# Pools by lifetime, and a later place for the forget gate's products: one edit of a hybrid attention/SSM block on one core

## The chip, the cores and the metric

The kernel runs on one core of a Trainium2 chip, as one program with one launch. A core has TensorE (PE in the profile; its weight loads are listed apart as PEld), VectorE (DVE), ScalarE (ACT), GpSimd (POOL) and SyncE (SP). SP and POOL issue most of the DMAs. The metric is device time in microseconds (us), the median over several runs of the same program; lower is better. The output has to agree with an fp32 reference.

## The reference, cut to what matters

One layer of a streaming encoder on 1024 frames of 1024 features, with 16 meta tokens put in front (1040 positions):

```python
xn = rmsnorm(h, norm_mix_g)
q, k, v, f_logit, u, gates = split(xn @ w_in, ...)    # 512, 512, 512, 8, 512, 2048 columns
y_a = forgetting_attention(q, k, v, f_logit, b_forget) @ w_attn_out
        # logit[t,s] = q_t.k_s/8 + F[t] - F[s],  F = cumsum(log_sigmoid(f_logit + b_forget))
z   = gelu(s5(u, ...))             # 32 groups of 16 channels, 64 complex states each
zg  = z @ w_glu                    # 512 -> 2048
y_s = zg[:, :1024] * sigmoid(zg[:, 1024:])
g   = sigmoid(gates)
h   = h + (g[:, :1024] * y_a + g[:, 1024:] * y_s) @ w_o
h   = h + conv_ffn(rmsnorm(h, norm_ffn_g))     # 1024 -> 2 x 2816 -> 1024, causal conv of width 3
out = rmsnorm(h, norm_final_g)[16:]
```

Everything is fp32. The edit concerns the first 300 us: the projection of `u`, the gates of the SSM branch, the SSM, the forget logits, q and k of the first head pair, and the loading of `z` for the GLU product.

## The kernel before, in words

**Products.** An fp32 operand is kept as a high part in the reduced type that PE takes at full rate and a low part with the rest; a product is three matmuls (high by high, high by low, low by high; `dense_steps`, lines 159 to 161). Features are `xhi` and `xlo`, 8 blocks of 128 features by 1040 positions. The high part is a cast or scaled copy on ACT (L369 for features, L146 and L603 for weights and z), the low part a subtraction (`split_lo`, L129, or the fused form in L370), mostly on DVE. `wchunk` (L138) streams a 1024 by 128 weight block through two buffers each of `raw`, `whi`, `wlo`; with `act=True` the cast is on ACT and the low part is made by an accumulating DMA, issued by POOL (`lo_by_dma`, L133 to 136). `seven` (L202) forms a product of 2 x 2 blocks with seven block products instead of eight; its weight forms are combined on POOL (L643) and split into buffer pairs `ops`, ten of them, that lie in the `whi`/`wlo` buffers (eight) and in the GLU's pool (two).

**Stages at issue.** (1) Normalization and `u`'s projection by four blocks of positions. The features of blocks 0 and 1 are first made without the norm's factor for `u`'s product; then `factors` and `normed_features` make the normalized ones for all blocks. `us`, four tiles of 128 channels, is scaled by the factor for the first two blocks (L436, four DVE operations) and stored to `u_d` in DRAM (L440, 32 DMAs on SP and POOL). (2) The gates of the SSM branch, chunks 8 to 15 of 16 (`gate_chunk`, `stage_gates`): 8 chunks x 3 pieces of positions x 24 matmuls = 576 matmuls; each piece is evicted with a sigmoid on ACT (L484) into a `gs` tile and stored to `g_d` by POOL (L485). (3) The SSM in four quarters of 8 groups. A quarter loads its `U` back from `u_d`, makes tables on DVE (`Vm`, `Wi`, `Gm`, `Kt`, `Tm`), multiplies `Wi` by `U` on PE (L1789), runs rotations and two scans on DVE (L1512, L1810, L1811) into states `St`, multiplies these with `Gm` and `U` with `Tm` on PE (L1830, L1832), applies the gelu on ACT and stores `Y` to `y_d` (L1835). The gate products are a generator: `advance(q)` emits them up to 288, 360, 480, 540 between the steps of the quarters, and `run(gates)` the last 36 after the SSM. (4) `forget()`: 3 pieces of 16 matmuls each, ACT copies to `fx` (L532), DVE adds into `fl_` (L533), then log sigmoid, a scan and a store. (5) `load_z`: for each quarter eight loads of `zt` from `y_d` (L598; half of the last quarter's on POOL), casts (L603) and splits into `zs`, and sums and differences `zf` on DVE and POOL (L616 to 619) whose casts and splits are the blocks T1 to T4. (6) q and k of the first head pair (`project_qk`, with `act=True`), then eight GLU blocks, each a `seven` followed by `gate`.

**Memory.** Pools are opened on a left and on a right stack of on-chip memory. A tile that lies where older tiles were waits, tile by tile, for their last users (`reuse_waits="tile"`). The SSM has one pool `sp` and an `sio` (for `sy` and `U`) on the left. `usb`, the tiles of `us`, are two in a pool `up` above and two in the `pc` slots. The gates' `gs` tiles lie on the right, in part over where `usb` lies. `forget` has a pool `fwork` on the right with `fl_` and `fx`, after the gates' pool is closed. `zt`, `zf` and the GLU's outputs share a pool `gated`, and all of z (`zs`, T1 to T3) with the GLU's work tiles a pool `glu`, both over the memory of the SSM.

**Order.** The order of the instructions on each engine isn't that of the program text: a planner simulates the kernel, and on each engine takes next what is ready by its own estimates, with the earlier in the text first. `after(inst, first)` adds an edge that fixes an order without a semaphore. The position of a step in the text is thus its priority.

The code itself:

Of the kernel before, what the change touches and what calls it, by code (L numbers as in the profile page):

```python
# [46 lines left out]
TILES = [(0, META)] + [(META + P * i, P) for i in range(SEQ // P)]  # L47


@with_exitstack  # L50
def block_kernel(ctx, tc, x, meta, xbt, x0t, g1t, w_q, w_k, w_v, w_f, w_u, w_g, b_f, w_ao, lam_d, bw_d, cw_d,
# [79 lines left out]
    late = []  # L131
# [6 lines left out]
    def wchunk(src, k, eng=None, act=False, copy=False):  # L138
# [6 lines left out]
        if act:  # L145
            S.copy(hi, raw)  # L146
            lo_by_dma(lo, hi, src)
            return hi, lo
# [17 lines left out]
    def run(gen):  # L166
        for _ in gen:
            pass
# [111 lines left out]
    sp = pool(st_s, "ssm", side="left")  # L280
    sio = pool(st_s, "ssmio", side="left")
    for tag, n, cols in (("Gm", 2, 1152), ("Tm", 2, 1024), ("Wi", 2, 1024), ("pc", 2, 2080), ("tq", 3, 1152)):
        sp.tile([P, cols], F, tag=tag, name="hold", bufs=n)
# [39 lines left out]
    for i in range(5, 9):  # L323
        load_x(i)
    us2, ul2 = (sp.tile([P, 2, n, SW if n == 2 else NCH], dt, tag="pc", name=nm, bufs=2)
                for n, dt, nm in ((CH, F, "usb"), (2, R, "ul")))
# [47 lines left out]
    def normed_features(b):  # L374
# [3 lines left out]
        return [features(b, k)[1] for k in range(KD)][-1]  # L378
# [37 lines left out]
    for b in (2, 3):  # L416
        last = normed_features(b)
# [8 lines left out]
        if b == 3:  # L426
            for q in (0, 1):
                factors(q)
            for q in (0, 1):
                normed_features(q)  # L430
# [3 lines left out]
    for m in range(4):  # L434
        ub = us[m][:, :, :rs01.shape[1] // CH]
        V.tensor_tensor(ub, ub, by_chunks(rs01), ALU.mult)  # L436
# [29 lines left out]
    split_lo(GP, wf[:, :, 32:32 + H], fraw, wf[:, :, :H])  # L466
    st_g = ExitStack()
# [4 lines left out]
    def gate_chunk(i, pl, tanh):  # L472
# [3 lines left out]
        for t, n in QBLK[::-1] if i == KD else QBLK:  # L476
# [5 lines left out]
            else:  # L482
                gs = pl.tile([P, LQ // 3], F, tag="gs", name="gs", bufs=2)
# [13 lines left out]
    BEHIND = (288, 360, 480, 540)  # L497
# [7 lines left out]

    st_x = ExitStack()
    sx = pool(st_x, "ssmx", side="left")
    begin(0)
    ssm_out(0)
    begin(1)  # L510
    for q in range(4):
        next(chains[q])
        if q < 3:
            ssm_out(q + 1, sx if q == 1 else None)
        advance(q)
        run(chains[q])
        if q < 2:
            begin(q + 2)
        if q == 1:
            next(ssm_steps)  # L520
    st_x.close()
    run(gates)
    st_g.close()
    st_s.close()
# [20 lines left out]
    fw = pool(st_f, "fwork", side="right")  # L545
    fl_, fx = (fw.tile([H, L], F, name=nm) for nm in ("fl_", "fx"))
    forget()
    st_f.close()
# [29 lines left out]
    gz = pool(st_k2, "gated", side="left")  # L578
    zp = pool(st_z, "glu", side="left")
    TH = L // 2  # L580
    NC2 = NCH // 2
    T3, T2, T1 = ([zp.tile([P, 2, TH], R, name=f"z{i}{w}") for w in "hl"] for i in (3, 2, 1))
# [1317 lines left out]
```

## Time and profile before

| what | value |
|---|---|
| median of 3 runs | 1477.25 us (1477.24 to 1478.09) |
| the profiled execution | 1479.76 us, span 1478.0 us |
| mean granted TensorE clock | 0.990 |
| PE busy | 1432.5 us (97%), 9646 matmuls |
| PEld busy | 1351.2 us (91%) |
| DVE busy | 1075.8 us (73%), 2198 instructions |
| ACT busy | 724.0 us (49%), 1419 instructions |
| POOL busy | 770.1 us (52%), 888 instructions |
| DMA | 209.31 MB, mean 142 GB/s |
| instructions | 26529 |

The profile is that of one execution. "Busy" is the time in which an engine had an instruction running. A table of windows gives for each stretch of the span the busy time and number of instructions of each engine, the granted clock of TensorE (1.00 is full), the mean busy share of the 16 DMA engines and the rate. A line of waits reads: waiting engine and line, the arrow and what released it, then total time, count and mean in us. A line of the timeline reads: start, duration, engine (SPq is SP's queue of DMA issues) and line, operation, outputs and inputs with shapes, number of instructions run together, and in brackets the idle time ahead of the first with its releaser.

### The profile page before, as it was taken

The numbers are of one execution on the slowest core, as the hardware profiler recorded it, in microseconds if no ns is written. First come the engines' busy times: TensorE is split into PE (matmuls) and PEld (weight loads), VectorE is DVE, ScalarE is ACT, GpSimd is POOL, SyncE is SP. The second block draws the span as 40 slices with busy tenths as digits, with TensorE's granted clock in tenths as the row PEclk, the third lists the DMA queues.
The fourth block names the chain that finished last, engine by engine and source line by source line (L and its number), as shares of the span: only waits on it lengthen the run. The fifth ranks groups of instructions, "written<-read, shape, count | busy, mean of one in ns | idle before, by whom it ended". The sixth has DMA issues, their size and how long they took to land. (4 is left out here: it accounts for less than half of the span.)

```text
span 1478.0 us, 26529 instructions
## 1 busy us (share of the span) xinstructions
PE 1432.5 (97%) x9646; PEld 1351.2 (91%) x9646; DVE 1075.8 (73%) x2198; ACT 724.0 (49%) x1419; POOL 770.1 (52%) x888
## 2 busy tenths in 40 slices
PE   8989997999999999999999999999999999998997
PEld 8889997998899999999879999999999999776886
DVE  7888758861657676656469977788877666788685
ACT  7556566531646565542655444444444445652433
POOL 2722128760646556515861244555544327889766
PEclk9999998999999999999999999999999999999998
DMA  8746553550027432146974255667753214866413
GB/s 309 174 116 162 140 115 100 168 159 32 25 74 197 108 80 94 44 177 237 274 156 143 66 141 145 168 174 195 185 136 107 79 69 154 306 200 168 135 40 114
DMA packets 89653, 209.31 MB, mean 142 GB/s; under 512 B 14442, under 2 KB 22266, under 8 KB 89140
## 3 DMA queue, kind: packets, MB, share of 16 engines
q1 hardware_dynamic: 70068, 162.55, 33.6%
q0 software_dynamic: 17728, 41.41, 14.5%
q10 hardware_dynamic: 1728, 3.68, 0.7%
q8 instruction: 76, 1.25, 0.4%
q14 instruction: 53, 0.43, 0.1%
HBM read 168.52 MB, written 69.35 MB: 161 GB/s over the span
## 5 line engine op out<-in xcount | busy, mean ns | idle before, releaser
L159 PE MATMUL mm<-xhi,whi 128*128 128x342 f32 (+2 forms) x480 | 157.8, 329 | 5.6 <-ACT gs L484 2.9
L161 PE MATMUL mm<-xhi,wlo 128*128 128x342 f32 (+2 forms) x480 | 156.3, 326 | 0.0
L160 PE MATMUL mm<-xlo,whi 128*128 128x342 f32 (+2 forms) x480 | 155.8, 325 | 0.0
L1135 POOL TENSOR_TENSOR ov<-ov,og 128x1024 f32<-128x1024 f32 x21 | 51.1, 2434 | 121.8 <-ACT og L1134 117.9
L129 DVE TENSOR_TENSOR sw<-sf,sw 128x512 fp32r<-128x512 f32 x72 | 66.7, 927 | 50.4 <-ACT sw L1126 50.2
L1126 ACT CAST sw<-sf 128x512 fp32r<-128x512 f32 x72 | 44.9, 624 | 108.8 <-POOL sf L1252 78.0
L159 PEld LDWEIGHTS mm<-xhi,whi 128*128 128x128 f32 x480 | 91.0, 190 | 7.2 <-ACT gs L484 3.2
L160 PEld LDWEIGHTS mm<-xlo,whi 128*128 128x128 f32 x480 | 91.0, 190 | 0.6 <-issue 0.4
L161 PEld LDWEIGHTS mm<-xhi,wlo 128*128 128x128 f32 x480 | 90.9, 189 | 0.6 <-issue 0.2
L819 ACT CAST th<-tp 128x256 fp32r<-128x256 f32 (+3 forms) x120 | 56.2, 472 | 62.1 <-PE tp L812 29.5
L1252 POOL TENSOR_TENSOR sf<-raw,sf 128x512 f32<-128x512 f32 x36 | 62.2, 1727 | 44.1 <-DVE sw L129 43.9
L1252 POOL TENSOR_TENSOR sf<-raw 128x512 f32<-128x512 f32 x36 | 48.2, 1338 | 68.8 <-DMA raw<-in_w_up_dram 29.3
L129 DVE TENSOR_TENSOR tl<-tp,th 128x256 fp32r<-128x256 f32 (+3 forms) x120 | 65.2, 547 | 25.3 <-ACT th L819 23.7
L223 PE MATMUL mm<-xhi,sw 128*128 128x258 f32 (+1 forms) x288 | 81.0, 281 | 0.0
L221 PE MATMUL mm<-xhi,sw 128*128 128x258 f32 (+1 forms) x288 | 80.8, 281 | 0.0
L222 PE MATMUL mm<-xlo,sw 128*128 128x258 f32 (+1 forms) x288 | 80.7, 280 | 0.0
L784 POOL TENSOR_SCALAR pt<-pt,nm 128x144 f32<-128x144 f32 (+4 forms) x72 | 52.3, 738 | 50.6 <-DVE nm L783 49.7
L1304 DVE SCALAR_TENSOR_TENSOR ov<-hv,cwt,ov 128x1024 f32<-128x1024 f32 x36 | 71.8, 1993 | 0.0
L1126 ACT CAST sw<-raw 128x512 fp32r<-128x512 f32 x70 | 43.0, 621 | 51.1 <-PE sp L223 23.2
L782 ACT ACTIVATE pt<-pt,nm 128x144 f32<-128x144 f32 (+4 forms) x72 | 52.9, 735 | 25.7 <-DVE nm L781 25.2
L775 DVE CUSTOM_DVE_ANT_0 pt<-sp,fb 128x328 f32<-128x328 f32 (+8 forms) x112 | 46.5, 430 | 21.4 <-PE sp L770 12.4
L129 DVE TENSOR_TENSOR sw<-raw,sw 128x512 fp32r<-128x512 f32 x70 | 55.9, 802 | 5.6 <-ACT sw L1126 4.9
(711 smaller groups left out, 5734.7 us busy)
## 6 DMA issues: line engine op xcount, KB each, us to landing
raw<-in_w_up_dram SPq DMA_DIRECT2D x44, 512.0 KB, 3.8
t_d<-in_w_dn_dram POOLq DMA_DIRECT2D x44, 256.0 KB, 6.8
ar<-a_d SPq DMA_DIRECT2D x44, 256.0 KB, 5.3
wr<-t_d SPq DMA_DIRECT2D x44, 256.0 KB, 2.8
a_d<-ov SPq DMA_DIRECT2D x21, 512.0 KB, 2.6
wr<-in_w_dn_dram SPq DMA_DIRECT2D x33, 256.0 KB, 4.3
t_d<-in_w_dn_dram SPq DMA_DIRECT2D x22, 256.0 KB, 4.3
t_d<-t_d SPq DMA_DIRECT2D x22, 256.0 KB, 4.9
```

The lines of the kernel that those rows point to most:

```text
L129: return eng.tensor_tensor(out_, src, hi.bitcast(F), ALU.subtract)
L159: yield PE.matmul(ps, whi[:, i, :], ahi[:, i], start=(i == 0), stop=False)
L160: yield PE.matmul(ps, whi[:, i, :], alo[:, i], start=False, stop=False)
L161: yield PE.matmul(ps, wlo[:, i, :], ahi[:, i], start=False, stop=(i == k - 1))
L221: PE.matmul(ps, a[0][:, i], bh, start=(i == 0 and not joins), stop=False, skip_group_check=True)
L222: PE.matmul(ps, a[0][:, i], bl, start=False, stop=False, skip_group_check=True)
L223: PE.matmul(ps, a[1][:, i], bh, start=False, stop=(i == kh - 1), skip_group_check=True)
L782: S.activation(pt[:n, :kc], pt[:n, :kc], AF.Exp, bias=nm[:n, 1:2], scale=0.125, accum_out=nm[:n, 2:3])
L819: S.copy(th[:kn, z:tw], tp[:kn, z:tw])
L1126: S.copy(hi, src)
L1252: sums.append(GP.tensor_tensor(f_, a, b, op))
L1304: V.scalar_tensor_tensor(out=o, in0=h_[:, j:SEQ + j], scalar=cwc(j, m), in1=o, op0=ALU.mult, op1=ALU.add)
```

## The change

The instructions are the same but for addresses, order edges and the place of two steps.

- A class `ByTag` hands each tile to a pool by its tag. The SSM's pool is now three: `ssma` (`Gm`, `Tm`), `ssmb` (the rest: `Wi`, `pc`, `tq`, `dg` and the small constants), `ssmc` (`wr`, `wi`, `ta`, `tb`, `dt8` and `pd`), and `ssmio` as before. Of the two `pc` buffers one becomes the tag `pd`. `gated` becomes three pools by tag (`ms`, `gl`, `cg`). z gets three pools: `za` with `zs[0]`, `zb` with T3, T2, T1, `zc` with `zs[1]`; `glu` keeps the GLU's work tiles.
- `forget()` is called after the last SSM output and after gate product 552, ahead of the last 24 gate products. `fl_` is a `sy` tile and `fx` a `Gm` tile of the small pool `ssmx`; the pool `fwork` is gone.
- The first gate chunk evicts into one `sy` tile, `g0s`, instead of three `gs` tiles.
- Order edges: the four scalings of `usb` come after the last `xlo` of block 1; the first DVE operation of the first output tables comes after it too; the ACT casts of gate chunks from the second on come after the last `xhi` copy of block 1.

```diff
@@ -47,6 +47,14 @@
 
+class ByTag:
+    def __init__(self, rest, **tags):
+        self.rest, self.tags = rest, tags
+
+    def tile(self, shape, dtype, tag, **k):
+        return self.tags.get(tag, self.rest).tile(shape, dtype, tag=tag, **k)
+
+
 @with_exitstack
@@ -128,7 +136,7 @@
 
-    late = []
+    late, n_act = [], [0]
 
@@ -143,7 +151,10 @@
         if act:
-            S.copy(hi, raw)
+            cast = S.copy(hi, raw)
+            if n_act[0]:
+                after(cast, late[1])
+            n_act[0] += 1
             lo_by_dma(lo, hi, src)
@@ -277,9 +288,9 @@
     st_s = ExitStack()
-    sp = pool(st_s, "ssm", side="left")
-    sio = pool(st_s, "ssmio", side="left")
-    for tag, n, cols in (("Gm", 2, 1152), ("Tm", 2, 1024), ("Wi", 2, 1024), ("pc", 2, 2080), ("tq", 3, 1152)):
+    sa, sb, sc, sio = (pool(st_s, "ssm" + n, side="left") for n in ("a", "b", "c", "io"))
+    sp = ByTag(sb, Gm=sa, Tm=sa, **{tag: sc for tag in ("wr", "wi", "ta", "tb", "dt8", "pd")})
+    for tag, n, cols in (("Gm", 2, 1152), ("Tm", 2, L), ("Wi", 2, 1024), ("pc", 1, 2080), ("tq", 3, 1152)):
         sp.tile([P, cols], F, tag=tag, name="hold", bufs=n)
@@ -322,8 +333,8 @@
         load_x(i)
-    us2, ul2 = (sp.tile([P, 2, n, SW if n == 2 else NCH], dt, tag="pc", name=nm, bufs=2)
-                for n, dt, nm in ((CH, F, "usb"), (2, R, "ul")))
+    us2, ul2 = (sp.tile([P, 2, n, SW if n == 2 else NCH], dt, tag=tag, name=nm, bufs=1)
+                for n, dt, tag, nm in ((CH, F, "pd", "usb"), (2, R, "pc", "ul")))
     ul = [sio.tile([P, 2, SW], R, tag="U", name="ul", bufs=2) for _ in range(2)] + [ul2[:, i] for i in range(2)]
@@ -375,7 +386,7 @@
             V.tensor_tensor(xT[b][q], xT[b][q], spread[b].unsqueeze(1).broadcast_to([P, 4, n]), ALU.mult)
-        return [features(b, k)[1] for k in range(KD)][-1]
+        return [features(b, k) for k in range(KD)][-1]
 
@@ -414,7 +425,7 @@
     for b in (2, 3):
-        last = normed_features(b)
+        last = normed_features(b)[1]
         if b == 2:
@@ -427,13 +438,14 @@
             for q in (0, 1):
-                normed_features(q)
+                cp_, last = normed_features(q)
+            late.append(cp_)
         for m in range(4):
...
         ub = us[m][:, :, :rs01.shape[1] // CH]
-        V.tensor_tensor(ub, ub, by_chunks(rs01), ALU.mult)
+        after(V.tensor_tensor(ub, ub, by_chunks(rs01), ALU.mult), last)
     for m in range(4):
@@ -464,6 +476,7 @@
     split_lo(GP, wf[:, :, 32:32 + H], fraw, wf[:, :, :H])
+    g0s = sio.tile([P, L], F, tag="sy", name="g0s", bufs=3)
     st_g = ExitStack()
@@ -480,7 +493,10 @@
             else:
-                gs = pl.tile([P, LQ // 3], F, tag="gs", name="gs", bufs=2)
+                if i == KD:
+                    gs = g0s[:, t:t + n]
+                else:
+                    gs = pl.tile([P, LQ // 3], F, tag="gs", name="gs", bufs=2)
                 S.activation(gs, ps[:, :n], AF.Sigmoid)
@@ -494,7 +510,7 @@
 
-    BEHIND = (288, 360, 480, 540)
+    BEHIND = (288, 360, 480, 540, 552)
     gates = stage_gates()
@@ -502,26 +518,6 @@
             n_gate[0] += 1
-
-    st_x = ExitStack()
-    sx = pool(st_x, "ssmx", side="left")
-    begin(0)
-    ssm_out(0)
-    begin(1)
-    for q in range(4):
-        next(chains[q])
-        if q < 3:
-            ssm_out(q + 1, sx if q == 1 else None)
-        advance(q)
-        run(chains[q])
-        if q < 2:
-            begin(q + 2)
-        if q == 1:
-            next(ssm_steps)
-    st_x.close()
-    run(gates)
-    st_g.close()
-    st_s.close()
 
@@ -542,9 +538,32 @@
 
-    fw = pool(st_f, "fwork", side="right")
-    fl_, fx = (fw.tile([H, L], F, name=nm) for nm in ("fl_", "fx"))
+    st_x = ExitStack()
+    sx = pool(st_x, "ssmx", side="left")
+    begin(0)
+    n_log = len(ssm_log)
+    ssm_out(0)
+    after(ssm_log[n_log], last)
+    begin(1)
+    for q in range(4):
+        next(chains[q])
+        if q < 3:
+            ssm_out(q + 1, sx if q == 1 else None)
+        advance(q)
+        run(chains[q])
+        if q < 2:
+            begin(q + 2)
+        if q == 1:
+            next(ssm_steps)
+    advance(4)
+    fl_ = sio.tile([P, L], F, tag="sy", name="fl_", bufs=3)[:H]
+    fx = sx.tile([P, 1152], F, tag="Gm", name="fx", bufs=1)[:H, :L]
     forget()
+    st_x.close()
+    run(gates)
+    st_g.close()
+    st_s.close()
+
     st_f.close()
@@ -575,12 +594,13 @@
     st_z, st_k2 = ExitStack(), ExitStack()
-    gz = pool(st_k2, "gated", side="left")
-    zp = pool(st_z, "glu", side="left")
+    gz = {n: pool(st_k2, "gated" + n, side="left") for n in ("ms", "gl", "cg")}
+    zqa, zqb, zqc = (pool(st_z, "z" + n, side="left") for n in "abc")
     TH = L // 2
     NC2 = NCH // 2
-    T3, T2, T1 = ([zp.tile([P, 2, TH], R, name=f"z{i}{w}") for w in "hl"] for i in (3, 2, 1))
-    zs = [[zp.tile([P, 2, L], R, name=f"z{w}{r}") for w in "hl"] for r in range(2)]
+    zs = [[pl.tile([P, 2, L], R, name=f"z{w}{r}") for w in "hl"] for r, pl in enumerate((zqa, zqc))]
+    T3, T2, T1 = ([zqb.tile([P, 2, TH], R, name=f"z{i}{w}") for w in "hl"] for i in (3, 2, 1))
+    zp = pool(st_z, "glu", side="left")
 
@@ -592,7 +612,7 @@
             tag = "gl" if m % 2 else "ms"
-            zt = gz.tile([P, CH, NCH], F, tag=tag, name="zt", bufs=2)
+            zt = gz[tag].tile([P, CH, NCH], F, tag=tag, name="zt", bufs=2)
             ym = y_d[m].rearrange("(j c) g n -> g c j n", c=GC)
@@ -611,7 +631,7 @@
         for k in range(2):
-            fa, fb = (gz.tile([P, L], F, tag="cg", name="zf", bufs=2) for _ in range(2))
+            fa, fb = (gz["cg"].tile([P, L], F, tag="cg", name="zf", bufs=2) for _ in range(2))
             f1, f2, f3, f4 = (fold(f_[:, TH * q:TH * q + TH]) for f_ in (fa, fb) for q in range(2))
@@ -626,7 +646,7 @@
     def glu(i):
-        gs = gz.tile([P, LQ], F, tag="gl", name="gl", bufs=2, padded_shape=[P, L])
+        gs = gz["gl"].tile([P, LQ], F, tag="gl", name="gl", bufs=2, padded_shape=[P, L])
         SY.dma_start(gs, g_d[D + P * i:D + P * i + P])
@@ -644,8 +664,8 @@
         A = weight_forms(raw[:, 0:2], raw[:, 2:4], raw[:, 4:6], raw[:, 6:8], combine, split_q)
-        ms = gz.tile([P, L], F, tag="ms", name="ms", bufs=2)
-        cg = gz.tile([P, L], F, tag="cg", name="cg", bufs=2)
+        ms = gz["ms"].tile([P, L], F, tag="ms", name="ms", bufs=2)
+        cg = gz["cg"].tile([P, L], F, tag="cg", name="cg", bufs=2)
         seven(zp, A, [zblock(0, 0), T3, T2, T1, zblock(1, 0), T4, zblock(1, 1)], 2,
@@ -691,7 +711,8 @@
         else:
-            raw = gz.tile([P, L], F, tag="gl" if q == 2 else "cg", name="raw", bufs=2)
+            t_ = "gl" if q == 2 else "cg"
+            raw = gz[t_].tile([P, L], F, tag=t_, name="raw", bufs=2)
             raw = raw[:, :2 * AW].rearrange("p (k m) -> p k m", k=2)
@@ -1515,7 +1536,7 @@
 
-    bufs = dict(Gm=2, Tm=2, Wi=2, U=2, tq=3, sy=3, wr=2, wi=2, dt8=1, ta=1, tb=1, pc=2, dg=1)
+    bufs = dict(Gm=2, Tm=2, Wi=2, U=2, tq=3, sy=3, wr=2, wi=2, dt8=1, ta=1, tb=1, pc=1, pd=1, dg=1)
 
@@ -1680,7 +1701,7 @@
         def rotation(h):
-            pc = big("pc", [P, 2, NH, NCH])
+            pc = big("pd" if h else "pc", [P, 2, NH, NCH], "pc")
             GP.memset(pc[:, 0, :, 0:1], 1.0)
@@ -1738,7 +1759,7 @@
             g0, bcx, bcp = views(qt)
-            Gm = pl.tile([P, GQ, CH + 1, GC], F, name="Gm") if pl else big("Gm", [P, GQ, CH + 1, GC])
+            Gm = pl.tile([P, GQ, CH + 1, GC], F, tag="Gm", name="Gm", bufs=1) if pl else big("Gm", [P, GQ, CH + 1, GC])
             tm = big("tq", [P, GQ, CH + 1, GC], "tm")
```

## The prediction

> **What bounds the kernel now.** I read the shares of the span first (PE is busy 97% of it), then the table by stages, then who PE waits for. PE is the bound, and only its holes can be won.
>
> ```profile
> core 0: us, PE busy (x) PEld busy (x) DVE busy (x) ACT busy (x) POOL busy (x), PEclk, DMA share, GB/s
> 60.00:80.00 20.00, 14.89 (x86) 14.60 (x87) 16.44 (x61) 3.28 (x6) 12.10 (x25) 0.94 0.97 202
> 80.00:100.00 20.00, 18.28 (x123) 17.11 (x123) 16.39 (x32) 8.79 (x18) 4.32 (x8) 0.97 0.40 105
> 160.00:180.00 20.00, 20.00 (x139) 20.00 (x138) 18.11 (x27) 10.64 (x16) 4.25 (x8) 1.00 0.52 131
> 180.00:200.00 20.00, 19.67 (x140) 18.22 (x138) 1.23 (x1) 7.93 (x11) 7.47 (x11) 1.00 1.01 216
> 200.00:222.00 22.00, 20.63 (x125) 20.63 (x126) 18.09 (x23) 18.93 (x27) 3.37 (x5) 1.00 0.17 44
> 222.00:240.00 18.00, 9.32 (x49) 8.54 (x48) 16.43 (x24) 10.91 (x27) 14.01 (x8) 0.72 0.27 88
> 240.00:300.00 60.00, 60.00 (x503) 60.00 (x502) 51.51 (x108) 32.76 (x85) 45.73 (x57) 1.00 0.47 141
> ```
>
> There are two holes near the change: 60 to 100 us (first gate block, start of the SSM) and 200 to 240 us (between the SSM and the first GLU block). In the second, DVE works 34.5 us of 40 just after it did nothing for 18.8 us of 20. That is work which came too late, not too much work: from 240 on PE is full. The waits of PE, over 0 to 150 us and then 150 to 430 us:
>
> ```profile
> PE mm L159 <- ACT gs L484: 2.9, 1, 2.9
> PE mm L160 <- DVE xlo L370: 2.5, 1, 2.5
> PE sp L1789 <- ACT Wi L1777: 1.7, 1, 1.7
> ...
> PE sp L223 <- DVE ops L129: 6.0, 1, 6.0
> PE mm L221 <- ACT c L230: 2.5, 1, 2.5
> PE mm L159 <- DVE fl__2342 L533: 1.7, 1, 1.7
> PE mm L221 <- DVE kl L129: 0.2, 1, 0.2
> ```
>
> So the late hole is 1.7 + 6.0 + 2.5 + 0.2 = 10.4 us of waiting, and a granted clock of 0.72 on 9.32 us of work in 222 to 240 (0.28 x 9.32 = 2.6 us): 13.0 us in all. The early one is 2.9 + 2.5 + 1.7 = 7.1 us, with 0.06 x 14.89 + 0.03 x 18.28 = 1.4 us of clock: 8.5 us.
>
> Why the late hole exists stands in the order of time of ACT, DVE, SP and PE:
>
> ```profile
> 177.07 1.42 DVE L1512 TENSOR_TENSOR St<-ta,wr 64x516 f32<-64x516 f32 x2
> 189.91 1.23 DVE L616 TENSOR_TENSOR zf<-zt 128x520 f32<-128x520 f32 x1 [11.42 <-DMA zt<-y_d]
> ...
> 200.42 1.12 ACT L532 COPY fx<-mm 8x272 f32<-8x272 f32 x3 [9.05 <-DMA g_d<-gs]
> 212.35 2.30 ACT L603 CAST zh<-zt 128x520 fp32r<-128x520 f32 x2
> ...
> 158.35 5.14 SPq L1762 DMA_DIRECT2D Tm<-Kt  x8
> 178.31 17.95 SPq L598 DMA_DIRECT2D zt<-y_d  x28
> ...
> 180.25 0.38 PE L1830 MATMUL tp<-St,Gm 128*128 128x130 f32 x2
> ```
>
> ACT stands 9.05 us on the forget gate's first copy, because `fx` lies on the right side where the gates' eviction tiles were, and their store must land first. z's first cast, ready at 189.9 by its data, runs at 212.35, behind all of forget and most of q: one pool holds all of z and the GLU's work tiles, and lies over `fl_` and `fx` too. Instructions wait tile by tile, but the planner that wrote the order began that pool only when everything under it was dead. The z loads start at 178.3 for the same kind of reason, although SP had nothing to issue since 163.5.
>
> **The change, part by part.**
>
> (1) z in six pools, SSM in four. No instruction is added or removed but for addresses. zt and the fold tiles now lie only over the pool of Wi, pc, tq and the small constants, dead once the last `Tm` loads are issued (158.35 + 5.14 = 163.5); zh0/zl0 over the same; the T forms over that and wr..tb, dead at 178.5; zh1/zl1 over `sy`. So the loads of the first two quarters leave SP 15 us sooner, into a stretch where the DMA share is 0.52 and not 1.01, and casts, splits and forms fall into the DVE gap of 180 to 200. The last quarter still hangs on the last SSM output.
>
> ```profile
> 187.07 0.54 POOL L1835 DMA_DIRECT2D y_d<-Y  x1 [5.54 <-ACT Y L1834]
> DMA to landing us min/median/max: 3.1/4.4/8.3
> L617 POOL TENSOR_TENSOR zf<-zt x2: 1312/4659/8006, 198.6 to 221.9; 128x520 f32<-128x520 f32 x2
> ```
>
> Store issued at 187.6, landed some 5 later, four loads on SP and four on POOL and 4.4 to land: about 199, then 7 us of casts, splits and forms: 206. PE needs it in the GLU's third product, after about 218. Slack about 12 us.
>
> (2) Forget moved ahead of the last 24 gate products, `fx` and `fl_` into SSM slots. It frees ACT of the 9.05 us and PE of the 1.7. `fl_` takes a `sy` slot, which the last but one SSM output has left by then. PE's sum stays. But the last gate piece now ends some 48 products later, and k's weights wait for its buffers (cast, low part, accumulating load):
>
> ```profile
> 163.02 0.32 PE L159 MATMUL po<-xhi,whi 128*128 128x342 f32 x1
> 166.79 0.32 PE L159 MATMUL mm<-xhi,whi 128*128 128x342 f32 x1
> ...
> 189.01 1.05 ACT L146 CAST whi<-raw 128x1024 fp32r<-128x1024 f32 x1 [0.46 <-PE po L160]
> 195.44 0.94 POOL L136 DMA_DIRECT2D wlo<-in_w_k_dram  x1
> DMA to landing us min/median/max: 6.0/7.0/8.4
> 209.94 0.28 PE L159 MATMUL mm<-xhi,whi 128*128 128x272 f32 x1
> ```
>
> 24 products take 3.77 us, 48 of them 7.5: cast at 196.5, low part 1 us later, issue 0.9, landing 7: 205.5 to 208. k's first product comes at 209.94 less what PE gains ahead of it (1.7, and what part 3 brings, 2.0): 206.2. So the old slack is used up. Between 0 and the 2.5 us by which 8.4 us of landing would miss it, I take 1.0. Behind that wait stand k's evictions and the first GLU block.
>
> (3) The first gate's evictions go to `g0s` in a `sy` slot. Before, the eviction tiles lay over `usb` and waited for its stores:
>
> ```profile
> 57.19 4.44 DVE L436 TENSOR_TENSOR usb<-usb,rsB 128x528 f32<-128x528 f32 x4
> 61.66 3.24 DVE L370 SCALAR_TENSOR_TENSOR xlo<-xT,g1T,xhi 128x256 fp32r<-128x256 f32 x8
> 58.48 16.04 SPq L440 DMA_DIRECT2D u_d<-usb  x16
> 74.44 1.28 ACT L484 ACT_TABLE_LOAD   x1 [8.46 <-DMA u_d<-usb]
> 74.52 1.36 DVE L1512 TENSOR_TENSOR Gm<-sm,sm 128x1152 f32<-128x1152 f32 x1 [3.52 <-DMA u_d<-usb]
> 97.97 0.28 DVE L1512 TENSOR_TENSOR Kt<-Kt,dg 16x128 f32<-16x128 f32 x1 [3.62 <-ACT Kt L1754]
> ```
>
> The 2.9 us go, with their clock. (4) `usb`'s scaling goes behind the eight `xlo`, and the second gate weights' cast behind the last `xhi`: PE's 2.5 us for `xlo` go. The price: the u_d stores, on SP and POOL, and the U loads behind them start 3.24 us later; the `Gm` of the third quarter waits for `usb`'s stores too, on DVE, with all tables behind it: 3.52 becomes 6.8, if the planner leaves it there. The next DVE wait (3.62, on `Kt`) takes that up.
>
> How much of the 8.5 arrives? PE begins the last SSM output at 180.25, and its last state is written at 177.07 + 1.42 = 178.5: DVE's chain is only 1.8 us ahead and nearly full (18.11 of 20). PE cannot be earlier there by more than 1.8 us plus what DVE gains, except where the order gives it gate or forget products in between. Ends: 3.2 lost (the late stores not taken up) and 8.5 gained. I take 2.0, nearest to the row that caps it.
>
> (5) First GLU. Its weights' splits (`ops`, the 6.0 wait) were late because DVE's queue was; two of its five buffer pairs come free only behind k. Left over: between 0 and the 2.5 of the row of `c`. I take 2.0.
>
> Sum: -13.0 + 2.0 + 1.0 - 2.0 = -12.0 us. The profiled execution is 1479.76 (span 1478.0 and 1.76 around it), so 1467.8 there; the median of the runs is 2.5 below it, so 1465.3.
>
> The Trainium skill, TensorE: Matmul & The Clock Gate (Part 1), has the clock fall to half after an idle window of about 3.4 us that runs free of the kernel. The trace agrees with the direction after the 6.0 us wait (0.72), and shows a dip after the 2.9 us wait as well (0.94 over 60 to 80), which is shorter than that window. By the rule, the waits of 1 and 2 us that I leave over would cost no clock: the sum stays. By the row they could cost up to 1.4 us more.
>
> **The rivals.**
>
> (a) All of it arrives: -13.0 - 8.5 = -21.5, 1455.8. For it: the planner can fill PE with products when the chain is late. Against it: it fills by its own times, and the 11.42 and 8.46 us waits show that it took the loads and stores for faster than they are.
>
> (b) z still late, by half. POOL's form took 1.3 us beside an idle DVE and 8.0 beside a full one. Twice 8.0 in the now dense DVE stretch is 13.4 us more, past the slack of 12 by 1.4; with POOL's own combinations of weights behind it (14.01 of 18 us busy in the hole) the 6.0 wait stays. -12.0 + 6.0 + 1.4 = -4.6: 1472.7. The Trainium skill's GPSIMD Engine Reference (1. Specifications) says that GpSimd shares its SBUF interfaces with VectorE and is held up by VectorE instructions with two SBUF inputs. It speaks for (b), and the rows of the form agree with it.
>
> (c) Slower. z's first form and splits, now allowed before the chain ends, are put in DVE's queue ahead of the fourth quarter's states and wait there for a load that the planner took for quick. Issue at 163.5, and from first issue to use it took 189.91 - 178.31 = 11.6: 175.1, while DVE comes free near 167.3: 7.8 us of waiting, and 1.23 + 3.07 of work = 12.1 on the chain. PE then waits 12.1 - 1.8 = 10.3, the clock costs its 2.6 again, and the gain of 11.0 less 1.0 stays: +2.9 and up, with the 2.0 of part 3 gone into the wait and z's last quarter 12 us later, its slack eaten: +4, 1481. It decides from about 8 us of delay on the chain.
>
> (d) The order stays as it was, pools or not: only forget's 1.7 and small parts: 1475, within 0.2% (3 us, about what a measurement can tell from no change).
>
> **How the numbers follow.** Forecast (1459 to 1470): 0.58. (a) 0.12, (b) 0.13, (c) 0.11, (d) 0.06. The range leaves out (c) and the upper part of (d): 1455.5 to 1475. Faster: 0.58 + 0.12 + 0.13 and a little of (d): 0.84; same 0.05; slower 0.11.
>
> **What would show it.** Right: first z load issued near 164; no wait of ACT on g_d at forget; zh cast before 195; PE without the 6.0 us wait, clock near 1.0 in 205 to 230; the first GLU product near 210; no wait of ACT on u_d before the first gate eviction. Wrong: DVE waiting on zt before the last `St`; PE waiting on `St`, on `wlo` of k, or on POOL's zf; a u_d wait on DVE longer than 3.5.

## The result, and the profile after

The changed kernel takes 1468.3 us, median of 6 runs (1465.48 to 1470.23), against 1477.24 us (1474.22 to 1478.09) of the kernel before on the same chip: ratio 0.9944, 95% interval 0.9929 to 0.9960. The forecast was 1465.3 (1455.5 to 1475.0). The profiled execution took 1469.97 us, 9.8 less than that of before.

Line numbers differ in the changed kernel: L159 to L161 are L170 to L172 now, L484 is L500, L598 is L618, L1512 is L1533, and the numbers of forget's lines are four lower (L532 is L528). The table by stages of the changed kernel (columns as in the prediction; the last row is a piece of the row of 200 to 222):

```profile
core 0: us, PE busy (x) PEld busy (x) DVE busy (x) ACT busy (x) POOL busy (x), PEclk, DMA share, GB/s
60.00:80.00 20.00, 20.00 (x129) 20.00 (x129) 20.00 (x55) 7.27 (x13) 11.98 (x22) 1.00 0.91 177
80.00:100.00 20.00, 20.00 (x139) 19.39 (x139) 18.17 (x39) 10.23 (x19) 8.99 (x17) 1.00 0.81 192
180.00:200.00 20.00, 19.71 (x131) 18.41 (x130) 9.71 (x11) 10.34 (x15) 5.06 (x6) 1.00 0.32 84
200.00:222.00 22.00, 14.59 (x77) 14.37 (x76) 17.73 (x18) 17.68 (x28) 9.29 (x7) 0.77 0.49 104
222.00:240.00 18.00, 18.00 (x144) 18.00 (x143) 13.24 (x30) 11.64 (x30) 11.52 (x16) 1.00 0.23 69
...
211.00:216.10 5.10, 5.10 (x22) 5.10 (x23) 5.04 (x5) 4.84 (x4) 3.09 (x4) 0.50 0.33 102
```

The early hole is gone altogether: PE is full from 60 to 100 us at full clock. The late hole is still there, only moved forward and under another name. The waits of PE from 150 to 300 us:

```profile
PE mm L172 <- DMA wlo<-in_w_k_dram: 7.4, 1, 7.4
PE tp L1851 <- DVE St L1533: 1.7, 1, 1.7
PE mm L170 <- DVE fl__2308 L529: 0.3, 1, 0.3
```

That is 9.4 us of waiting, and 5.10 us of work at half clock behind it, which costs 2.6: 12.0 us, where before had 13.0. So the late stretch gives 1.0 and the early one all of its 8.5; together 9.5 of the 9.8 us.

The timeline shows how k's weights came late, and why PE waited for `St` (start, duration, engine, line):

```profile
168.11 1.22 DVE L636 TENSOR_TENSOR zf<-zt 128x520 f32<-128x520 f32 x1 [0.65 <-DMA zt<-y_d]
169.40 1.27 DVE L137 TENSOR_TENSOR zl<-zt,zh 128x520 fp32r<-128x520 f32 x1
176.60 1.10 DVE L137 TENSOR_TENSOR zl<-zt,zh 128x520 fp32r<-128x520 f32 x1 [0.98 <-ACT zh L623]
177.74 1.42 DVE L1533 TENSOR_TENSOR St<-ta,wr 64x516 f32<-64x516 f32 x2
...
185.13 1.21 DVE L638 TENSOR_TENSOR zf<-zt,zf 128x520 f32<-128x520 f32 x1 [4.77 <-DMA zt<-y_d]
186.43 0.63 ACT L643 CAST z2h<-zf 128x520 fp32r<-128x520 f32 x1 [5.30 <-DVE zf L638]
189.17 0.37 ACT L1854 COPY Y<-tp 128x260 f32<-128x260 f32 x1
191.12 1.28 ACT L1855 ACT_TABLE_LOAD   x1
192.42 1.07 ACT L1855 ACTIVATE Y<-Y 128x1040 f32<-128x1040 f32 x1
193.51 0.84 ACT L528 COPY fx<-mm 8x384 f32<-8x384 f32 x2
196.49 1.28 ACT L532 ACT_TABLE_LOAD   x1 [2.14 <-DVE fx L531]
198.76 1.04 ACT L154 CAST whi<-raw 128x1024 fp32r<-128x1024 f32 x1
203.95 1.04 ACT L143 ACTIVATE wlo<-whi 128x1024 fp32r<-128x1024 f32 x1
211.72 4.07 ACT L623 CAST zh<-zt 128x1040 fp32r<-128x1040 f32 x2 [0.26 <-POOL fx L536]
...
205.29 0.92 POOL L144 DMA_DIRECT2D wlo<-in_w_k_dram  x1 [2.85 <-ACT wlo L143]
...
211.00 0.59 PE L172 MATMUL mm<-xhi,wlo 128*128 128x272 f32 x1 [7.41 <-DMA wlo<-in_w_k_dram]
```

The last gate product starts at 191.1, so k's cast could run from then on. But on ACT the gelu of the last SSM output, forget's copies and its exponential, which waits 2.14 us for DVE, stand ahead of it: the cast runs at 198.76. Between the cast and the low part (203.95) stand a gate's sigmoid and forget's logarithm with a table load of 1.28 us each.

The gelu is itself late. PE starts the last product of that SSM output at 182.22, but among ACT's copies of it (the last at 189.17) stand four casts of z's early work, and the first of them waits 5.30 us for a form on DVE that waits 4.77 us for its load. The table load ahead of the gelu comes 12.0 us behind the last states (191.12 and 179.16); in the kernel before it came 5.9 behind them (184.41 and 178.49). On DVE too, z's first form and two splits stand ahead of the last states, with their waits: 0.65 + 1.22 + 1.27 + 0.98 + 1.10 = 5.2 us.

### The profile page after: what moved, and what is told of

Same layout as the page of the kernel before. It is cut to its first block, busy times and chain, and to the rows that moved or that the text cites. A ratio compares the mean times of both kernels' runs of the same rounds, so it can differ in the third digit from the quotient of the medians.

```text
span 1467.7 us, 26536 instructions
## 1 busy us (share of the span) xinstructions
PE 1430.3 (97%) x9646; PEld 1350.7 (92%) x9646; DVE 1074.6 (73%) x2198; ACT 723.1 (49%) x1419; POOL 760.7 (52%) x888
## 5 line engine op out<-in xcount | busy, mean ns | idle before, releaser
L172 PE MATMUL mm<-xhi,wlo 128*128 128x342 f32 (+2 forms) x488 | 159.4, 327 | 7.4 <-DMA wlo<-in_w_k_dram 7.4
L170 PE MATMUL mm<-xhi,whi 128*128 128x342 f32 (+2 forms) x488 | 160.1, 328 | 1.3 <-DVE q L137 1.0
L172 PEld LDWEIGHTS mm<-xhi,wlo 128*128 128x128 f32 x488 | 92.9, 190 | 8.0 <-DMA wlo<-in_w_k_dram 7.6
L170 PEld LDWEIGHTS mm<-xhi,whi 128*128 128x128 f32 x488 | 93.0, 191 | 2.4 <-PE sp L791 0.8
```

The lines of the kernel that those rows point to most:

```text
L170: yield PE.matmul(ps, whi[:, i, :], ahi[:, i], start=(i == 0), stop=False)
L172: yield PE.matmul(ps, wlo[:, i, :], ahi[:, i], start=False, stop=(i == k - 1))
```

## The experiments

Each kernel was timed in 5 rounds beside the kernel before, on the same chip; ratios are to that. "PE's waits" are the longest, up to three, of the profiled execution from 150 to 300 us; "k's load" is the time at which POOL issues the accumulating load of k's low weights (205.29 in the changed kernel, 195.44 before), "last `St`" the end of the last states (179.16; before 178.49).

| kernel | median us | ratio, 95% interval | last `St` | k's load | PE's waits |
|---|---|---|---|---|---|
| changed | 1468.3 | 0.9944 [0.9929, 0.9960] | 179.16 | 205.29 | wlo 7.4, St 1.7 |
| c: early parts undone | 1476.46 | 1.0001 [0.9992, 1.0010] | 182.17 | 210.14 | wlo 7.3, fl_ 1.1, St 1.1 |
| j: edges undone | 1473.12 | 0.9984 [0.9971, 0.9997] | 182.65 | 208.50 | q 3.8, wlo 3.5, St 2.2 |
| d: early parts alone | 1465.4 | 0.9924 [0.9907, 0.9941] | 172.24 | 184.14 | ops 3.6, c 2.5 |
| b: z's pools joined | 1465.86 | 0.9919 [0.9906, 0.9933] | 172.13 | 194.88 | z2h 2.8, ops 1.9, wlo 1.5 |
| a: forget put back | 1469.16 | 0.9955 [0.9940, 0.9970] | 176.62 | 193.05 | q 3.2, St 2.0, ops 1.9 |
| g: k ahead of forget's tail | 1466.99 | 0.9937 [0.9923, 0.9950] | 176.84 | 197.69 | wlo 2.6, St 2.4, q 2.1 |
| h: z behind the last states | 1465.48 | 0.9923 [0.9910, 0.9937] | 172.82 | 202.79 | wlo 7.3 |
| l: fl_ apart from z | 1467.34 | 0.9936 [0.9922, 0.9950] | 176.38 | 203.39 | wlo 7.3, St 1.7 |
| m: g, h and l together | 1465.05 | 0.9915 [0.9899, 0.9931] | 171.63 | 198.72 | wlo 6.6 |
| p: a, h and l together | 1467.5 | 0.9932 [0.9920, 0.9944] | 171.27 | 192.28 | q 4.7, gs 2.9 |
| q: m, z also behind k | 1466.04 | 0.9925 [0.9912, 0.9937] | 171.12 | 193.98 | q 8.9, fl_ 1.6 |
| s: z cut in two around q | 1468.47 | 0.9946 [0.9931, 0.9961] | 173.20 | 185.07 | kl 3.4, q 1.8 |

### Where the gain comes from

**c, parts 3 and 4 undone.** The first gate evicts into `gs` again, and the three order edges are taken out.

```diff
-            if n_act[0]:
-                after(cast, late[1])
...
-                if i == KD:
-                    gs = g0s[:, t:t + n]
-                else:
-                    gs = pl.tile([P, LQ // 3], F, tag="gs", name="gs", bufs=2)
+                gs = pl.tile([P, LQ // 3], F, tag="gs", name="gs", bufs=2)
...
-        after(V.tensor_tensor(ub, ub, by_chunks(rs01), ALU.mult), last)
+        V.tensor_tensor(ub, ub, by_chunks(rs01), ALU.mult)
...
-    after(ssm_log[n_log], last)
```

> The changed kernel without the first gate's slot g0s and without the three order edges (parts 3 and 4 undone). Theory 1 (the early hole's 8.5 us arrive whole, because the DVE chain moves with it): the waits of 2.9, 2.5 and 1.7 us between 60 and 100 us come back with their clock, and PE's wait for k's weights does not absorb them, because its date follows PE's own products: 1468.3 + 8 = 1475 to 1477 us. Rival (the prediction's step: the chain on DVE lets only 2.0 us of them through): 1470 to 1471 us.

1476.46 us, the time of before: theory 1 holds. PE's waits of c from 40 to 150 us are nearly those of before again:

```profile
PE mm L169 <- DVE xlo L379: 2.5, 1, 2.5
PE mm L168 <- ACT gs L494: 2.2, 1, 2.2
PE sp L1803 <- ACT Wi L1791: 1.7, 1, 1.7
```

So without parts 3 and 4, parts 1 and 2 together bring nothing that these runs can measure.

**j, only the order edges undone.** `g0s` stays.

```diff
-            if n_act[0]:
-                after(cast, late[1])
...
-        after(V.tensor_tensor(ub, ub, by_chunks(rs01), ALU.mult), last)
+        V.tensor_tensor(ub, ub, by_chunks(rs01), ALU.mult)
...
-    after(ssm_log[n_log], last)
```

> The changed kernel without the three order edges (part 4); the slot g0s (part 3) stays. Theory (slot and edges each take away their own wait): the wait for xlo near 61 us comes back, 2.5 us, and some of the delay of the tables; the wait for the first eviction stays away: 1470 to 1473 us. Rival (the slot alone brings the gain, the edges nothing): 1467 to 1469 us.

1473.12 us, a tenth above what the theory gave and outside the rival's range. From 40 to 150 us PE waits for `xlo` (2.5, as before) and for `U` (1.7), and not for the first eviction. By the ratios, the slot alone brings 0.0016 x 1477 = 2.4 us, and the edges the other 5.9 of the changed kernel's 8.3; j's interval makes it 0.4 to 4.3 for the slot.

**d, parts 3 and 4 alone,** on pools, z and forget as before; of part 1 only the tag `pd` stays.

```diff
...
-    advance(4)
-    fl_ = sio.tile([P, L], F, tag="sy", name="fl_", bufs=3)[:H]
-    fx = sx.tile([P, 1152], F, tag="Gm", name="fx", bufs=1)[:H, :L]
-    forget()
     st_x.close()
     run(gates)
     st_g.close()
     st_s.close()
+    fw = pool(st_f, "fwork", side="right")
+    fl_, fx = (fw.tile([H, L], F, name=nm) for nm in ("fl_", "fx"))
+    forget()
...
-    zqa, zqb, zqc = (pool(st_z, "z" + n, side="left") for n in "abc")
+    zp = pool(st_z, "glu", side="left")
```

> The kernel before with parts 3 and 4 alone (slot g0s, three order edges); SSM and z pools and forget() as before. Theory (after the first four runs: parts 3 and 4 bring the whole gain, 8 us and more, parts 1 and 2 together none): 1467 to 1470 us, the waits between 60 and 100 us gone, those of 1.7, 6.0 and 2.5 us after 199 us still there. Rival (the early gain reaches the end only because z and forget moved too; alone it is held up by the chain on DVE): 1473 to 1476 us, a wait for St or U before 185 us.

1465.4 us: all of the gain, and more than expected. Of the three late waits that were expected to stay, the one of 6.0 us is 3.6, the one of 2.5 is there, and the 1.7 us for `fl_` are gone without part 2. The late waits of PE in d, and from its timeline the last states and the store of the last SSM output:

```profile
PE sp L234 <- DVE ops L137: 3.6, 1, 3.6
PE mm L232 <- ACT c L241: 2.5, 1, 2.5
```

```profile
170.82 1.42 DVE L1532 TENSOR_TENSOR St<-ta,wr 64x516 f32<-64x516 f32 x2
180.48 0.54 POOL L1855 DMA_DIRECT2D y_d<-Y  x1 [6.57 <-ACT Y L1854]
```

The last states end at 172.24 instead of 178.49, and the last SSM output is stored at 180.48 instead of 187.07. The rival, that DVE's chain holds the early gain up, falls: the chain moved by 6.3 us. What held it up in the kernel before can be read in DVE's waits from 60 to 100 us, first of before, then of d:

```profile
DVE Kt L1512 <- ACT Kt L1754: 3.6, 1, 3.6
DVE Gm L1512 <- DMA u_d<-usb: 3.5, 1, 3.5
```

```profile
DVE Gm L1532 <- DMA u_d<-usb: 1.0, 1, 1.0
DVE ta L1532 <- ACT wr L1812: 0.5, 1, 0.5
```

7.1 us of waiting there became 1.5 (1.7 in the changed kernel), which is 5.6 of the 6.3 us. The chain was full of work, but not free of waits.

**b, part 1 undone.** One SSM pool beside `ssmio`, `gated` and `glu` as before; forget ahead, `g0s`, the edges and the tag `pd` stay.

```diff
...
-    gz = {n: pool(st_k2, "gated" + n, side="left") for n in ("ms", "gl", "cg")}
-    zqa, zqb, zqc = (pool(st_z, "z" + n, side="left") for n in "abc")
+    gz1 = pool(st_k2, "gated", side="left")
+    gz = {n: gz1 for n in ("ms", "gl", "cg")}
+    zp = pool(st_z, "glu", side="left")
...
```

> The changed kernel without part 1: one SSM pool, one gated pool, one pool for z and the GLU's work tiles; forget() ahead, g0s and the edges stay. Theory (z's early casts are worth something, and k's late weights hide it): z's first cast runs behind forget's last use of fl_, near 212 us, the first GLU block waits 4 to 8 us for z or its weight splits, on top of the wait for k's weights: 1472 to 1477 us. Rival (the wait for k's weights gives z the time): 1467 to 1470 us.

1465.86 us. z's first cast runs at 196.24, not near 212. The first GLU block waits 2.8 us for `z2h` and 1.9 for `ops`, as the theory said, but not on top of the wait for k's weights, which is 1.5 us instead of 7.4. So the theory's time falls, and the rival's range lies above the result as well. Without the new pools the last states end at 172.13, as in d: z's early work no longer stands ahead of them.

Nor does it stand ahead of the gelu on ACT, whose table load runs at 177.45, 5.3 us behind the last states. forget is still ahead of k's cast and between cast and low part, as in the changed kernel, but all of it 10.4 us earlier:

```profile
188.36 1.03 ACT L154 CAST whi<-raw 128x1024 fp32r<-128x1024 f32 x1
193.54 1.04 ACT L143 ACTIVATE wlo<-whi 128x1024 fp32r<-128x1024 f32 x1
```

So part 1, by z's early work, has a share in the 7.4 us wait about as large as that of forget's place (g, below). It isn't z's work ahead of the last states alone that makes it: in h, below, these end as early as in b, z's casts stay early on ACT, and the wait stays at 7.3 us.

**a, forget back behind the last gate product,** all else as changed.

```diff
-    advance(4)
+    run(gates)
     fl_ = sio.tile([P, L], F, tag="sy", name="fl_", bufs=3)[:H]
     fx = sx.tile([P, 1152], F, tag="Gm", name="fx", bufs=1)[:H, :L]
     forget()
     st_x.close()
-    run(gates)
```

> The changed kernel, with forget() put back behind the last gate product (its tiles stay in the SSM's slots, all pools and edges stay). Theory 1 (k's low weights come late because the forget gate's work on ACT stands ahead of k's cast): the last gate piece ends 48 products earlier, k's cast stands ahead of forget's copies again, PE's 7.4 us wait for wlo of k goes, and with it some 3 us of clock; a wait of up to 1.7 us for fl_ comes back: 1468.3 - 10.8 + 1.7 = about 1459 us. Rival (z or the weight splits of the first GLU block are as late as k's weights were, and take the wait over): PE waits 6 us or more for ops or z instead, 1464 to 1469 us.

1469.16 us: the theory falls, and the time is just above the rival's range, without the single wait of 6 us that the rival named. k's load goes out at 193.05 and nobody waits for it, but PE waits for a free accumulator instead (`q`, whose splits on DVE stand behind z's and forget's scan), for `St` and for the first GLU block's weights, 10.2 us in six waits.

### What stands in the late hole

**g, k's low weights ahead of forget's exponential.** forget's tail comes behind q's and k's weights in the text, and its exponential is ordered behind k's low part.

```diff
...
+    tail = forget()
+    next(tail)
     run(gates)
+    qkw = [wchunk(w_[0], KD, GP, act=True) for w_ in (w_q, w_k)]
+    run(tail)
...
-        S.activation(fx, fx, AF.Exp, scale=-1.0)
+        after(S.activation(fx, fx, AF.Exp, scale=-1.0), lows[-1])
```

> The changed kernel with one thing more: forget's tail comes in the text behind q's and k's weights, and its first exponential on ACT is ordered behind the low part of k's weights. Theory 1: the low part of k leaves ACT before 199 instead of 205 us, its accumulating load lands before PE needs it near 203.6, the 7.4 us wait and 3.4 us of clock go: 1457 to 1461 us. Rival (the first GLU block's splits or z's last quarter are the next wait, just behind): a wait of 4 us or more for ops, c or z between 205 and 225 us, 1463 to 1468 us.

The wait for `wlo` falls from 7.4 to 2.6 us, so forget's place on ACT took 4.8 us of it. Together with b this shows two causes that do not add up: to take away either leaves 1.5 or 2.6 us. The time, 1466.99 us, lies in the rival's range, but none of the waits is the rival's of 4 us or more, and it isn't separated from the time of the changed kernel: `St` 2.4, `q` 2.1 and `kl` 1.4 take the place.

**h, z's work on DVE behind the last states.**

```diff
+    st_last = ssm_log[-1]
     advance(4)
...
-            split_lo(V, zl, zts[m][:, :, :w_], zh)
+            after(split_lo(V, zl, zts[m][:, :, :w_], zh), st_last)
...
-            V.tensor_tensor(f1, part(0, 1, k), part(0, 0, k), ALU.subtract)
+            after(V.tensor_tensor(f1, part(0, 1, k), part(0, 0, k), ALU.subtract), st_last)
```

> The changed kernel with z's work on DVE ordered behind the last SSM states. Theory 1: PE's 1.7 us wait for St goes, but k's weights come as late as before (their date hangs on forget's place on ACT), so at most those 1.7 us are won: 1466 to 1468.5 us. Rival (the 5.2 us that z's form and splits take of the DVE chain delay gelu, forget and so k's cast): all of it moves up by 4 to 5 us, 1463 to 1464.5 us.

The last states end at 172.82, 6.3 us earlier, PE no longer waits for them, and the wait for `wlo` stays at 7.3. 1465.48 us lies between the two theories: k's load moved up by 2.5 us, not by 0 and not by 5. z's casts are still on ACT, now among forget's copies, and the first of them waits 3.62 us for DVE.

**l, `fl_` in a `Tm` slot.** In the changed kernel `fl_` lies under `zh1` and `zl1`, so z's second half waits for forget's end (the row of 211.72 above).

```diff
-    fl_ = sio.tile([P, L], F, tag="sy", name="fl_", bufs=3)[:H]
+    fl_ = sp.tile([P, L], F, tag="Tm", name="fl_", bufs=2)[:H]
```

> The changed kernel with fl_ in a Tm slot, which lies under q and k and not under the second half of z. Theory: the casts of z's third and fourth quarter no longer wait for forget's scan (211.7 us), they run near 200 and 205 us; but PE waits for k's weights meanwhile, so alone it wins at most 1 us: 1467 to 1468.5 us. Rival: these casts (2.1 us each on ACT) stand ahead of the low part of k's weights, and the 7.4 us wait grows by 2 to 4 us: 1470 to 1472 us.

As the theory said: the last of these casts ends at 205.05 instead of 215.79, and 1467.34 us is no measurable difference, with the same 7.3 us wait for `wlo`.

### Can the hole be closed?

**m, the three edits of g, h and l together.**

> The changed kernel with all three: the low part of k's weights ahead of forget's exponential on ACT, z's work on DVE behind the last states, fl_ in a Tm slot. Theory (three waits stand one behind the other: St, k's weights, z's second half with the splits behind it, and each hides the next): PE waits less than 3 us in all from 150 to 300 us, 1456 to 1459 us. Rival (the splits of the first GLU block's weights on DVE and POOL are next): a wait of 3 us or more for ops or c, 1460 to 1463 us.

1465.05 us, above both ranges. The wait for `wlo` is 6.6 us again. Two queues hold k's load up, ACT's and POOL's:

```profile
194.88 2.43 ACT L628 CAST zh<-zt 128x1040 fp32r<-128x1040 f32 x1 [0.20 <-issue]
196.99 1.17 ACT L143 ACTIVATE wlo<-whi 128x1024 fp32r<-128x1024 f32 x1
...
195.15 3.06 POOL L642 TENSOR_TENSOR zf<-zt 128x520 f32<-128x520 f32 x1 [4.27 <-DMA zt<-y_d]
198.13 0.59 POOL L501 DMA_DIRECT2D g_d<-gs  x1
198.72 0.96 POOL L144 DMA_DIRECT2D wlo<-in_w_k_dram  x1
```

On ACT a cast of z stands between k's cast (191.86) and its low part, which ends at 198.16. On POOL z's form, which waits 4.27 us for its load, stands ahead of k's load and ends at 198.21. Either alone would have held the load until 198.

**q, m with z's last two casts and the second form also ordered behind k's low part and its load.**

```diff
-            S.copy(zh, zts[m][:, :, :w_])
+            zc_ = S.copy(zh, zts[m][:, :, :w_])
+            if m > 1:
+                after(zc_, lows[-2])
...
-            GP.tensor_tensor(f3, part(1, 1, k), part(0, 1, k), ALU.subtract)
+            f3_ = GP.tensor_tensor(f3, part(1, 1, k), part(0, 1, k), ALU.subtract)
+            if k:
+                after(f3_, lows[-1])
```

Here `lows` holds k's low part on ACT and its load on POOL.

> As m_all (low part of k's weights ahead of forget's exponential, z's work on DVE behind the last states, fl_ in a Tm slot), and also z's casts of the third and fourth quarter on ACT, and the second form on POOL, ordered behind the low part of k's weights and its load. Theory (in m_all the 6.6 us wait stayed because two casts of 2.3 us each and POOL's form stood ahead of k's low part and its load): the load is issued near 194.5 instead of 198.7 us, the wait falls to 2 us or less with its clock, 1459 to 1462 us. Rival (something else is as late as k's weights): 1464 to 1466 us.

k's load is issued at 193.98 and its wait falls to 0.6 us, as the theory said, but the time, 1466.04 us, is the rival's. PE waits longer, for an accumulator:

```profile
212.41 0.66 PE L170 MATMUL po<-xhi,whi 128*128 128x384 f32 x1 [8.92 <-DVE q L137]
```

The product of q's first split was there since 191. Its cast on ACT ran at 204.80, and on DVE the split, at 211.37, stands behind z's second half and forget's scan.

**p, the three edits of a, h and l together.**

> The changed kernel with forget() put back behind the last gate product, z's work on DVE behind the last states, and fl_ in a Tm slot. Theory (in the changed kernel z's work delays the last states, forget delays k's weights on ACT, and fl_ delays the second half of z; each of the three is taken away): PE waits 3 us or less from 150 to 300 us, 1458 to 1462 us. Rival (the splits of q, k and of the first GLU block's weights bound the stretch from 200 to 230 us whatever stands ahead of them): another wait of 3 us or more, for q, ops or c, 1464 to 1467 us.

1467.5 us, just above the rival's range: again a wait for q's splits (4.7) and one for a gate's eviction (2.9).

**s, z cut in two,** on p, with the weights of q and k ahead of forget in the text: z's first half on ACT and POOL behind k's low weights, its second half on DVE behind q's splits. `load_z` yields after the first half, and q's products come between.

```diff
...
-    T4 = load_z()
+    z_steps = load_z()
+    T4 = next(z_steps)
     qk = qk_tiles(0)
-    run(project_qk(0, qk))
+    pq = project_qk(0, qk)
+    for _ in range(6 * KD * 3 // 2 + 1):
+        next(pq)
+    run(z_steps)
+    run(pq)
...
-            V.tensor_tensor(f1, part(0, 1, k), part(0, 0, k), ALU.subtract)
+            after(V.tensor_tensor(f1, part(0, 1, k), part(0, 0, k), ALU.subtract), q_last[-1] if k else st_last)
```

> The changed kernel with forget() behind the last gate product, fl_ in a Tm slot, the weights of q and k allocated ahead of forget's work, and z's work cut in two: its first half on DVE behind the last states and on ACT and POOL behind the low part and the load of k's weights, its second half on DVE behind q's splits. Theory (what z gains by coming early it loses by standing ahead of the last states and of q's splits on DVE; where it stands behind both, it fills DVE's idle 12 us between the last states and forget, and the first GLU block has its operands in time): no wait of PE above 3 us from 150 to 300 us, 3 to 6 us below the run with parts 3 and 4 alone: 1459 to 1462 us. Rival (the hole between SSM and GLU has a floor near what parts 3 and 4 leave): 1464 to 1467 us, with a wait of another name.

1468.47 us, above the rival's range. DVE has z's first half done by 190.5 and forget's first steps by 192.3, and then stands idle:

```profile
199.98 1.23 DVE L534 SCALAR_TENSOR_TENSOR fx<-fl__2353,fx 8x1040 f32<-8x1040 f32 x1 [7.70 <-ACT fx L533]
...
195.18 2.29 ACT L626 CAST zh<-zt 128x1040 fp32r<-128x1040 f32 x1 [0.45 <-DMA zt<-y_d]
197.50 1.28 ACT L533 ACT_TABLE_LOAD   x1
```

This step of forget on DVE waits 7.7 us for its logarithm on ACT, and q's splits stand behind it. 4.8 us of that are forget's own exponential and logarithm with a table load each; the other 2.7 or so are z's cast and its short wait for a load. The changed kernel has a wait of 7.7 us at the same step, there with k's cast and a gate's sigmoid in between.

All eleven kernels with parts 3 and 4, the changed one among them, lie between 0.9915 and 0.9955, whatever is done to z, forget and k. Each order of the late stretch took one wait away and got another. Whether some order closes the hole stays open; four attempts did not. The simplest of the fastest is d, parts 3 and 4 alone: 1465.4 us, which beats the kernel before (ratio 0.9924). Its median is 2.9 us below the changed kernel's, but the two intervals overlap: that parts 1 and 2 do harm beside parts 3 and 4 is suggested and not shown.

## Why the prediction was right, and where it was wrong

The size and the sign came out (-8.9 for -12.0), but that is luck: two steps failed in opposite directions. The early term was -2.0 and measured -8.5; the late terms were -13.0 + 2.0 + 1.0 = -10.0 and measured -1.0.

- **Part 3 and 4, "PE cannot be earlier there by more than 1.8 us plus what DVE gains": failed in its size.** The sum took DVE's gain as next to nothing. DVE gained 6.3 us at the last states (d), of which 5.6 are its own waits. The forecast had these two waits, 3.52 and 3.62 us, in its rows, but let the first grow and the second only make up for that. The term of 2.0 measured 8.5 in the early stretch of the profiles, 8.2 by the medians of c and the changed kernel, and d's whole gain is 11.2 by its ratio. The upper end of its range was the truth, and the row that seemed nearest was the wrong one. The price of the later `u_d` stores, 3.2 us, did not appear: from 60 to 100 us DVE waits for no store in the changed kernel, and 1.0 us in d.
- **Late hole, "-13.0": only the names went.** The waits for `ops` and `c` are gone, as forecast, and the 1.7 for `fl_` became 0.3, but k's weights took their place.
- **Part 2, k's weights, "cast at 196.5, low part 1 us later": the wait was named, its reason and size were wrong.** The term of 1.0 (0 to 2.5) was 7.4 us of waiting and 2.6 of clock, 10.0. The forecast reckoned with k's buffer alone, which was free from 191.4. ACT's queue was left out: z's early casts ahead of the gelu (b, without them, keeps 1.5 us of the wait), and forget, whose exponential stands ahead of k's cast and whose logarithm stands between the cast and the low part (g, with both behind, keeps 2.6). A second slip is in the sum itself: it reckons 2 us from cast to load, while its rows have 6.4 (189.01 to 195.44); the changed kernel has 6.5.
- **Part 1, z.** The first load was issued at 161.44, forecast near 164. The last casts were forecast done before 206 and ended at 215.79. Missed: `fl_` in a `sy` slot lies under z's second half (l). It cost nothing that can be measured, because k was later still. Missed too: what z's early casts do to ACT's queue while they wait for their loads.
- **Part 5.** The 2.0 left over were not seen: the first GLU block stood behind k, and its weights were ready.
- **Rival (a)** had the early gain right (-8.5) and the late one wrong. **Rival (b)**: POOL's forms took 2.35 and 3.78 us in the changed kernel, not 8.0; it did not happen there. In b, with z late again, one took 8.68. **Rival (c)** happened in small: z's work stands ahead of the last states on DVE, 5.2 us, and in h they end 6.3 us earlier. The same mechanism struck on ACT, which the rival did not name. It did not make the kernel slower, because the chain had become 6.3 us faster at the same time; the forecast weighed it against a slack of 1.8. **Rival (d)** fell: the order changed, with z's first load 17 us earlier (161.44 for 178.31).
- Of the signs named: the first z load, `zh` cast before 195 (168.10), no wait of ACT on g_d, none on u_d ahead of the first gate's eviction (it moved to the second chunk's, 6.9 us, where PE doesn't wait for it), and no 6.0 us wait came as forecast; the clock near 1.0 and the first GLU product near 210 did not (0.50 from 211 to 216, and 224.73). DVE waiting on `zt` before the last `St` (0.65 us) and PE waiting on `St` and on k's `wlo` were named as signs of an error, and they were.

The Trainium skill, TensorE: Matmul & The Clock Gate (Part 1), has the clock halve after an idle window of about 3.4 us. The trace agrees behind the 7.4 us wait: 0.50 from 211.0 to 216.1, then 0.98 up to 222 and 1.00.

## What to carry to other kernels

A chain on one engine that looks full in a table of busy time can still hold waits: list that engine's own waits in the stretch before capping a gain by it. When a step is moved forward, look at the queue of every engine that it passes, not only at the buffer that it frees or holds: here the cost sat on ACT, where z's casts waited ahead of the SSM's last output, and where forget's steps stood ahead of k's cast and between the cast and its low part. Undo the parts one by one before explaining a total: a forecast can be near the measured time by luck, with both of its main terms wrong.

## What the runs showed that was not expected

A short wait can cost clock or not. From 60 to 80 us PE waits once in j, for 2.5 us, and twice in c, for 2.5 and 2.2 us; yet the rows of that stretch show a lower clock in j alone (first j, then c). Each is one execution, and why they differ stays open:

```profile
60.00:80.00 20.00, 17.50 (x104) 17.33 (x103) 18.12 (x63) 5.08 (x10) 13.57 (x26) 0.91 0.99 203
```

```profile
60.00:80.00 20.00, 15.30 (x96) 15.01 (x96) 17.17 (x62) 3.64 (x7) 12.21 (x25) 1.00 0.94 191
```

The runs of one kernel spread further than the first three of before (0.85 us) led one to think: before from 1473.73 to 1479.03 in 17 runs, m from 1461.23 to 1467.65 in 6. Differences of 2 to 3 us between kernels of this study are at the edge of what 5 rounds tell.
